# The shift of the second norm added on TensorE for two token tiles, and a routing product moved to ScalarE

## The chip, the cores and the metric

The kernel runs on one core of a Trainium2 chip. The metric is the device time of one execution in microseconds (us). Five engines run their own instruction streams in order and wait for one another through semaphores: TensorE (PE, with its weight loads shown apart as PEld), VectorE (DVE), ScalarE (ACT), GpSimd (POOL) and SyncE (SP), which issues most DMAs. PE writes only to PSUM banks; DVE and ACT read them.

## What is computed

Two layers of an encoder over 1024 tokens of width 1024, all in float32. Each layer: a norm, a projection, attention and a linear recurrence side by side, an output projection with a gated residual; then a second norm, a router that picks two of 32 experts for every token, and the experts. The part that matters here, from the reference:

```python
x = x + gt1 * mixed
h2 = rms_norm(x, norm2_g[l]) * (1.0 + sc2) + sh2
x = x + gt2 * hier_moe(h2, moe_w_group[l], moe_b_group[l], moe_w_router[l], moe_b_router[l],
                       moe_w_gate[l], moe_w_up[l], moe_w_down[l])
...
g_top, g_idx = lax.top_k(g_prob, 1)
in_group = e_logits[jnp.arange(T), g_idx[:, 0]]
top_v, top_i = lax.top_k(in_group, TOP_K)
```

`sh2` is one row of 1024 numbers, the same for every token.

## The kernel before

The 1024 tokens are eight tiles of 128 tokens (tile 0 to 7), one token to a partition. In each layer a long stage, the mix (projection, attention, recurrence), is followed by the output projection and the routing (`out_proj`, L1350 on), and then by a loop over the experts (`moe`). This document speaks mostly of the stage between the mix and the experts, which runs once in each layer: about 930 to 1010 us in layer 0 and 2202 to 2283 us in layer 1.

In it the last output products (`out_product`, tile `po`, 24 matmuls into two PSUM banks for each tile and half of the inner dimension) are added to the residual `xm` by DVE (L1342), and ACT squares the sum for the norm (L1344). For each token tile `logits` transposes `xm` on PE (L1377, tile `n2_xT_ps`), ACT copies that to SBUF (L1378), PE multiplies by the router's weights (L1380, tile `pl`, 36 columns) and DVE copies the result to `lg` (L1381). `norms` makes the reciprocal root on DVE (L1385 and L100 to L109). `scale` finishes the logits (L1390, L1391). `finish` makes the normed row itself, `h2`: DVE multiplies (L1395), DVE adds the shift (L1396), and ACT's queue issues the DMA to `h2d` in DRAM (L1397). The shift needs no place in the logits, since `router_weights` folds it into their bias ahead of time.

Routing goes by four tiles at a time. `route_select` picks two experts for each token with some 25 short DVE instructions and two ACT exponentials (L1489, L1498); its result is the one-hot `r_oh`. `route_rank` counts tokens for each expert with two PE matmuls into `r_pc` (L1515, L1516), turns the counts into ranks (L1518, L1519), multiplies `r_oh` by the token codes and by the weights (L1522, both on DVE, tile `r_rhs`) and sums them with eight pairs of a DVE comparison (L1528, tile `r_ohr`, four buffers) and a PE matmul (L1529, tile `r_pv`); L1530 adds that to the table `r_tab`. `route_tables` turns the table into index lists (L1537 to L1541). Then POOL gathers the rows of the first expert from `h2d` (L1665), PE transposes them (L1673), and the expert loop begins.

Tiles 6 and 7 come last: their logits, norm and rows are made while the ranks of tiles 0 to 3 are still being made, and the selection and ranking of tiles 4 to 7 stand alone at the end.

PSUM: `tp` has two banks (transposes), `po` four (output products), `pl` two, which `pl`, `r_pc` and `r_pv` share in turn.

Order: each engine runs its instructions in the order in which a scheduler put them when the program was built. The scheduler takes the code's order as priority and places an instruction where its own estimate of the engines' times finds it ready. So an edit at one place can change the order elsewhere. In the expert loop the order is fixed by `in_order`.

Of the kernel before, what the change touches and what calls it, by code (L numbers as in the profile page):

```python
# [10 lines left out]
F32 = mybir.dt.float32  # L11
# [3 lines left out]
AF = mybir.ActivationFunctionType  # L15
OP = mybir.AluOpType
# [36 lines left out]
class Trunk:  # L53
# [1309 lines left out]
    def out_proj(self, l, side, psum, early, late):  # L1363

        nc, a = self.nc, self.a
        with ExitStack() as s:
            tp = s.enter_context(self.pool(name=f"tO{l}", bufs=2, side=side))
            wr, br = self.wr, self.br

            def logits(t):  # L1370
                pl = psum.tile([128, 36], F32, name="pl", tag="pl")
                xT = tp.tile([128, 8, 128], F32, name="n2_xT", tag="n2_xT")
                for g in range(2):
                    pt = psum.tile([128, 4, 128], F32, name="n2_xT_ps", tag="tp")
                    for k in range(4):
                        c = 512 * g + 128 * k
                        nc.tensor.transpose(pt[:, k, :], self.xm[:, t, c:c + 128], self.ident)  # L1377
                    nc.scalar.copy(xT[:, 4 * g:4 * g + 4, :], pt)  # L1378
                for k in range(NK):
                    nc.tensor.matmul(pl, xT[:, k, :], wr[:, k, :], start=(k == 0), stop=(k == NK - 1))  # L1380
                nc.vector.tensor_copy(self.lg[:, t, :], pl)  # L1381

            def norms(t, n):
                ss = tp.tile([128, n], F32, name="n2_s", tag=f"n2_s{n}")
                nc.vector.tensor_tensor(ss, self.ss[:, t:t + n, 0], self.ss[:, t:t + n, 1], op=OP.add)  # L1385
                return self.rsqrt(tp, ss, n, NORM_EPS, 1.0 / D, "n2")

            def scale(t, n, rs):
                lg = self.lg[:, t:t + n, :]
                nc.vector.tensor_tensor(lg, lg, rs.unsqueeze(2).to_broadcast([128, n, 36]), op=OP.mult)  # L1390
                nc.vector.tensor_tensor(lg, lg, br.unsqueeze(1).to_broadcast([128, n, 36]), op=OP.add)  # L1391

            def finish(t, rs):
                h2 = tp.tile([128, D], F32, name="h2", tag="h2", bufs=4)
                nc.vector.scalar_tensor_tensor(h2, self.xm[:, t, :], rs, self.g2, op0=OP.mult, op1=OP.mult)  # L1395
                nc.vector.tensor_add(h2, h2, self.sh2)  # L1396
                nc.scalar.dma_start(self.h2d[128 * t:128 * t + 128, :], h2)  # L1397

            self.route_init(self.mx)
            early()  # L1400
            parts = self.out_parts(psum, [(t, 0) for t in range(4, NT)])

            def more(n):
                for _ in itertools.islice(parts, n):
                    pass

            more(4)
            for t, n in enumerate((4, 4, 5, 5)):
                logits(t)
                more(n)  # L1410
            rs = norms(0, 4)
            scale(0, 4, rs)
            for t in range(4):
                finish(t, rs[:, t:t + 1])
                if t == 1:
                    logits(4)
                    more(10)
            logits(5)
            rs = norms(4, 2)
            scale(4, 2, rs)  # L1420
            self.route_select(0, tp)
            more(99)
            self.route_rank(0, tp, psum)
            for i in range(2):
                finish(4 + i, rs[:, i:i + 1])
            logits(6)
            logits(7)
            late()
            rs = norms(6, 2)
            scale(6, 2, rs)  # L1430
            self.route_select(4, tp)
            for i in range(2):
                finish(6 + i, rs[:, i:i + 1])
            self.route_rank(4, tp, psum)
            pool = self.mx
            self.idx_s = pool.tile([128, 48], I32, name="idx_s")
            self.idx_g = pool.tile([128, 48], I32, name="idx_g")
            self.wsl = pool.tile([128, 48], F32, name="wsl")
            self.ovf = pool.tile([1, 16], I32, name="ovf")
            self.routed = self.route_tables(self.R["tab"], slice(0, 32), tp)  # L1440
# [65 lines left out]
    def route_rank(self, t, w, psum, k=4):  # L1506

        nc, R = self.nc, self.R
        tt = slice(t, t + k)
        oh = w.tile([128, k, 32], F32, name="r_sum", tag="r_sum", bufs=1)  # L1510
        nc.vector.tensor_add(oh, R["oh"][:, tt, 0, :], R["oh"][:, tt, 1, :])
        for i in range(k):
            nc.vector.tensor_add(R["acc"][:, t + i + 1], R["acc"][:, t + i], oh[:, i])
        pc = psum.tile([128, k, 32], F32, name="r_pc", tag="pl")
        nc.tensor.matmul(pc, R["ups"], oh, start=True, stop=False)  # L1515
        nc.tensor.matmul(pc, R["ones"], R["acc"][:, tt, :], start=False, stop=True)  # L1516
        tmp = w.tile([128, k, 2, 32], F32, name="r_tmp", tag="r_tmp", bufs=1)
        nc.vector.tensor_tensor(tmp, R["oh"][:, tt], pc.unsqueeze(2).to_broadcast([128, k, 2, 32]), op=OP.mult)  # L1518
        nc.vector.tensor_reduce(R["rk"][:, tt, :].unsqueeze(3), tmp, axis=AX.X, op=OP.add)  # L1519
        rhs = w.tile([128, k, 2, 64], F32, name="r_rhs", tag="r_rhs", bufs=1)  # L1520
        for j, n in enumerate(("code", "wt")):
            nc.vector.tensor_tensor(rhs[:, :, :, 32 * j:32 * j + 32], R["oh"][:, tt],  # L1522
                                                    R[n][:, tt].unsqueeze(3).to_broadcast([128, k, 2, 32]), op=OP.mult)
        pv = psum.tile([128, 64], F32, name="r_pv", tag="pl")
        for i in range(k):
            for c in range(2):
                ohr = w.tile([128, 128], F32, name="r_ohr", tag="r_ohr", bufs=4)
                nc.vector.tensor_scalar(ohr, R["io"], R["rk"][:, t + i, c:c + 1], None, op0=OP.is_equal)  # L1528
                nc.tensor.matmul(pv, ohr, rhs[:, i, c, :], start=(i + c == 0), stop=(i + c == k))  # L1529
        nc.vector.tensor_add(R["tab"], R["tab"], pv)  # L1530
# [472 lines left out]
```

## Time and profile before

| | us |
|---|---|
| median of 3 runs | 2689.37 |
| the runs | 2685.37, 2689.37, 2702.67 |
| the profiled execution, its own time | 2696.09 |
| its span from first to last instruction | 2694.1 |
| PE busy / DVE busy / ACT busy over the span | 2389.1 / 1852.7 / 1193.2 |

A row of a timeline gives start, duration, engine, line, operation, output and inputs with the size, how many instructions it merges, and in brackets how long the engine was idle before it and what released it. One float32 matmul of the program shows as two records of PE. [...] PE's instructions overlap, so that a row's duration is longer than the distance from its start to the next start.

### The profile page before, as it was taken

The numbers are of one execution on the slowest core, as the hardware profiler recorded it, in microseconds if no ns is written. First come the engines' busy times: TensorE is split into PE (matmuls) and PEld (weight loads), VectorE is DVE, ScalarE is ACT, GpSimd is POOL, SyncE is SP. The second block draws the span as 40 slices with busy tenths as digits, with TensorE's granted clock in tenths as the row PEclk, the third lists the DMA queues.
The fourth block names the chain that finished last, engine by engine and source line by source line (L and its number), as shares of the span: only waits on it lengthen the run. The fifth ranks groups of instructions, "written<-read, shape, count | busy, mean of one in ns | idle before, by whom it ended". The sixth has DMA issues, their size and how long they took to land. (4 is left out here: it accounts for less than half of the span.)

```text
span 2694.1 us, 45448 instructions
## 1 busy us (share of the span) xinstructions
PE 2389.1 (89%) x17313; PEld 1826.6 (68%) x17313; DVE 1852.7 (69%) x4053; ACT 1193.2 (44%) x2316; POOL 313.7 (12%) x251
## 2 busy tenths in 40 slices
PE   6999998898889979999959989989997996999992
PEld 3666666777767866777736767767776885677771
DVE  4347767656579486877764588965658847787775
ACT  3344443234256224555545555424426622555552
POOL 3100000000000002333310000000000001333330
PEclk8998998789989979999979989899988997999996
DMA  8566765525354247999942434445336325899985
GB/s 295 175 214 205 211 210 166 155 91 148 93 171 126 95 171 290 354 338 359 369 174 103 147 113 143 141 140 166 117 89 193 104 97 195 319 385 348 336 307 202
DMA packets 263940, 542.68 MB, mean 201 GB/s; under 512 B 76504, under 2 KB 180896, under 8 KB 234784
## 3 DMA queue, kind: packets, MB, share of 16 engines
q1 hardware_dynamic: 235712, 484.61, 53.9%
q0 software_dynamic: 23376, 40.99, 4.1%
q10 hardware_dynamic: 4624, 14.06, 1.4%
q8 instruction: 141, 2.31, 0.4%
q14 instruction: 87, 0.71, 0.1%
HBM read 459.29 MB, written 120.09 MB: 215 GB/s over the span
## 5 line engine op out<-in xcount | busy, mean ns | idle before, releaser
L1646 DVE TENSOR_TENSOR w_lo<-w_gu,w_hi 128x2048 fp32r<-128x2048 f32 x134 | 306.3, 2286 | 69.2 <-ACT w_hi L1645 69.0
L1645 ACT CAST w_hi<-w_gu 128x2048 fp32r<-128x2048 f32 x134 | 255.7, 1908 | 211.2 <-PE h_ps L1698 204.5
L361 PE MATMUL pj<-hh,wa_hi 128*128 128x512 f32 x800 | 335.2, 419 | 2.1 <-ACT wa_hi L348 1.7
L362 PE MATMUL pj<-hl,wa_hi 128*128 128x512 f32 x800 | 332.2, 415 | 1.1 <-DVE hl L338 1.0
L363 PE MATMUL pj<-hh,wa_lo 128*128 128x512 f32 x800 | 325.5, 408 | 0.1
L1737 PE MATMUL y_ps<-w_d,hT 128*128 128x512 f32 x560 | 252.2, 593 | 3.4 <-ACTq L1798 2.4
L1697 PE MATMUL h_ps<-w_hi,xT_hi 128*128 128x512 f32 x560 | 243.0, 434 | 4.4 <-ACT xT_hi L1681 4.4
L1698 PE MATMUL h_ps<-w_hi,xT_lo 128*128 128x512 f32 x560 | 222.6, 398 | 2.5 <-DVE xT_lo L1682 2.5
L1699 PE MATMUL h_ps<-w_lo,xT_hi 128*128 128x512 f32 x560 | 222.4, 397 | 0.0
L1726 POOL DMA_INDIRECT yd<-yo,idx_s x70 | 183.6, 2623 | 290.2 <-DVE yo L1723 275.4
L361 PEld LDWEIGHTS pj<-hh,wa_hi 128*128 128x128 f32 x800 | 156.2, 195 | 41.5 <-issue 6.0
L362 PEld LDWEIGHTS pj<-hl,wa_hi 128*128 128x128 f32 x800 | 155.8, 195 | 37.0 <-issue 4.0
L363 PEld LDWEIGHTS pj<-hh,wa_lo 128*128 128x128 f32 x800 | 155.2, 194 | 35.4 <-issue 3.6
L1737 PEld LDWEIGHTS y_ps<-w_d,hT 128*128 128x128 f32 x560 | 100.9, 190 | 104.8 <-issue 100.4
L1697 PEld LDWEIGHTS h_ps<-w_hi,xT_hi 128*128 128x128 f32 x560 | 107.3, 192 | 38.0 <-issue 11.5
L1698 PEld LDWEIGHTS h_ps<-w_hi,xT_lo 128*128 128x128 f32 x560 | 107.3, 192 | 36.7 <-DVE th L1689 11.5
L1682 DVE TENSOR_TENSOR xT_lo<-xT_ps,xT_hi 128x1024 fp32r<-128x1024 f32 x70 | 85.7, 1225 | 65.8 <-ACT xT_hi L1681 65.8
L1699 PEld LDWEIGHTS h_ps<-w_lo,xT_hi 128*128 128x128 f32 x560 | 107.0, 191 | 23.0
L1723 DVE SCALAR_TENSOR_TENSOR yo<-y_ps,wsl,gt 128x1024 f32<-128x1024 f32 x70 | 89.8, 1283 | 38.3 <-PE y_ps L1737 38.3
L1192 ACT ACTIVATE at_p<-at_s,at_mx 128x256 f32<-128x256 f32 (+7 forms) x128 | 94.8, 741 | 40.6 <-DVE at_mx L1190 39.8
L1190 DVE TENSOR_REDUCE at_mx<-at_s 128x1 f32<-128x256 f32 (+7 forms) x128 | 95.6, 752 | 14.5 <-PE at_s L1188 13.3
L238 PE MATMUL ada_ps<-ada_w,crep 128*32 128x128 f32 x1536 | 71.9, 313 | 37.6 <-DMA ada_w<-in_ada_w 37.4
(436 smaller groups left out, 4949.3 us busy)
## 6 DMA issues: line engine op xcount, KB each, us to landing
w_gu<-in_moe_w_gu SPq DMA_DIRECT2D x140, 1024.0 KB
w_d<-in_moe_w_down SPq DMA_DIRECT2D x70, 1024.0 KB
ada_w<-in_ada_w SPq DMA_DIRECT2D x96, 512.0 KB
wa_raw<-in_w_in SPq DMA_DIRECT2D x50, 512.0 KB
sp_z<-z SPq DMA_DIRECT2D x32, 768.0 KB
b_zz<-sp_z SPq DMA_DIRECT2D x32, 512.0 KB
cy<-yd SPq DMA_DIRECT2D x16, 1024.0 KB
qkv<-qst SPq DMA_DIRECT2D x48, 256.0 KB
```

The costliest lines, as they stand in the source:

```text
L361: nc.tensor.matmul(ps, hi[:, k, :], self.hh[k][:, sl], start=(k == 0), stop=False)
L362: nc.tensor.matmul(ps, hi[:, k, :], self.hl[k][:, sl], start=False, stop=False)
L363: nc.tensor.matmul(ps, lo[:, k, :], self.hh[k][:, sl], start=False, stop=(k == NK - 1))
L1190: nc.vector.tensor_reduce(mx, ps[:, 0:n], axis=AX.X, op=OP.max, negate=True)
L1192: nc.scalar.activation(pm[:, 0:n], ps[:, 0:n], AF.Exp, bias=mx, accum_out=hs["s"][:, t, m:m + 1])
L1645: self.nc.scalar.copy(hi, raw)
L1646: eng.tensor_tensor(lo, raw, hi.bitcast(F32), op=OP.subtract)
L1697: nc.tensor.matmul(ph, hi[:, k, :], whi[:, k % 4, :], start=(k == 0), stop=False)
L1698: nc.tensor.matmul(ph, lo[:, k, :], whi[:, k % 4, :], start=False, stop=False)
L1699: nc.tensor.matmul(ph, hi[:, k, :], wlo[:, k % 4, :], start=False, stop=(k == NK - 1))
L1726: st = nc.gpsimd.indirect_dma_start(out=self.yd, out_offset=bass.IndirectOffsetOnAxis(ap=self.idx_s[:, e:e + 1], axis=0), in_=yos[e % 2], ...
L1737: nc.tensor.matmul(po[:, 512 * half:512 * half + 512], hT[:, k, :], w[:, k, 512 * half:512 * half + 512], start=(k == 0), stop=(k == 1))
```

## The change

Two edits, in both layers.

First, in `finish`: for tiles 6 and 7 DVE no longer adds the shift. For each half of 512 columns PE forms in a `po` bank the product of a row of ones and the row `sh2` (one partition deep), adds the product of the identity and `h2` to it, and ACT copies the bank back into `h2`.

Second, in `route_rank` for tiles 4 to 7: the product of the one-hot and the codes is made by eight ACT instructions of 128x32 in place of one DVE instruction of 128x256.

```diff
             def finish(t, rs):
                 h2 = tp.tile([128, D], F32, name="h2", tag="h2", bufs=4)
                 nc.vector.scalar_tensor_tensor(h2, self.xm[:, t, :], rs, self.g2, op0=OP.mult, op1=OP.mult)
-                nc.vector.tensor_add(h2, h2, self.sh2)
+                if t < 6:
+                    nc.vector.tensor_add(h2, h2, self.sh2)
+                else:
+
+                    for half in range(2):
+                        cs = slice(512 * half, 512 * half + 512)
+                        po = psum.tile([128, 512], F32, name="n2_h", tag="po")
+                        nc.tensor.matmul(po, self.R["ones"][0:1, :], self.sh2[0:1, cs], start=True, stop=False)
+                        nc.tensor.matmul(po, self.ident, h2[:, cs], start=False, stop=True)
+                        nc.scalar.copy(h2[:, cs], po)
                 nc.scalar.dma_start(self.h2d[128 * t:128 * t + 128, :], h2)
...
         for j, n in enumerate(("code", "wt")):
-            nc.vector.tensor_tensor(rhs[:, :, :, 32 * j:32 * j + 32], R["oh"][:, tt],
-                                                    R[n][:, tt].unsqueeze(3).to_broadcast([128, k, 2, 32]), op=OP.mult)
+            if t and n == "code":
+                for i in range(k):
+                    for c in range(2):
+                        nc.scalar.activation(rhs[:, i, c, 0:32], R["oh"][:, t + i, c, :], AF.Copy, scale=R[n][:, t + i, c:c + 1])
+            else:
+                nc.vector.tensor_tensor(rhs[:, :, :, 32 * j:32 * j + 32], R["oh"][:, tt],
+                                        R[n][:, tt].unsqueeze(3).to_broadcast([128, k, 2, 32]), op=OP.mult)
```

What the scheduler made of it. The text calls the new matmuls by ones and `sh2` the shift matmuls (L1403 after) and those by the identity the identity matmuls (L1404 after); the lines of the changed kernel are 9 to 14 higher from here on. First place, PE in layer 0 near the end of the output products, where `po_10316` and `po_10331` are the last two banks of products and `n2_xT_ps` is a transpose for tile 5. Before:

```order
L1336 MATMUL po_10331<-wo_0at_q0_9212,mT_10194 128x512
L1337 MATMUL po_10331<-wo_0at_q1_9213,mT_10194 128x512
L1377 MATMUL n2_xT_ps_10243<-ident_86,xm_8653 128x128 x4
L1338 MATMUL po_10316<-wo_0at_q0_9212,mT_10194 128x512
L1336 MATMUL po_10316<-wo_1at_k0_9274,mT_10194 128x512
```

After:

```order
L1336 MATMUL po_10331<-wo_0at_q0_9212,mT_10194 128x512
L1337 MATMUL po_10331<-wo_0at_q1_9213,mT_10194 128x512
L1403 MATMUL n2_h_10521<-sh2_8667,r_ones_9937 128x512
L1403 MATMUL n2_h_10525<-sh2_8667,r_ones_9937 128x512
L1377 MATMUL n2_xT_ps_10243<-ident_86,xm_8653 128x128 x4
L1338 MATMUL po_10316<-wo_0at_q0_9212,mT_10194 128x512
L1336 MATMUL po_10316<-wo_1at_k0_9274,mT_10194 128x512
```

The two shift matmuls of tile 6 now stand inside the last output products.

Second place, PE in layer 0 right behind the last output product: the transposes of tile 6 (`n_xT_ps`), the two count matmuls into `r_pc`, the rank matmuls into `r_pv`, and the logits `pl` of tile 6. Before:

```order
L1377 MATMUL n_xT_ps<-ident,xm 128x128 x8
L1515 MATMUL r_pc<-r_sum,r_ups 128x128
L1516 MATMUL r_pc<-r_acc,r_ones 128x128
L1529 MATMUL r_pv<-r_rhs,r_ohr 128x64 x7
L1380 MATMUL pl<-wr,n_xT 128x36 x3
```

After:

```order
L1377 MATMUL n_xT_ps<-ident,xm 128x128 x2
L1524 MATMUL r_pc<-r_sum,r_ups 128x128
L1377 MATMUL n_xT_ps<-ident,xm 128x128 x6
L1403 MATMUL n_h<-sh,r_ones 128x512
L1525 MATMUL r_pc<-r_acc,r_ones 128x128
L1543 MATMUL r_pv<-r_rhs,r_ohr 128x64 x4
L1380 MATMUL pl<-wr,n_xT 128x36 x4
```

Six transposes and a shift matmul of tile 7 now stand between the two count matmuls, and only four rank matmuls ahead of the first logits.

Third place, PE in layer 0 from there to the next count matmul: the last eight rows of `pl` are the logits of tile 7. Before:

```order
L1529 MATMUL r_pv<-r_rhs,r_ohr 128x64
L1380 MATMUL pl<-wr,n_xT 128x36
L1377 MATMUL n_xT_ps<-ident,xm 128x128 x4
L1380 MATMUL pl<-wr,n_xT 128x36 x4
L1377 MATMUL n_xT_ps<-ident,xm 128x128 x4
L1380 MATMUL pl<-wr,n_xT 128x36 x8
```

After:

```order
L1377 MATMUL n_xT_ps<-ident,xm 128x128 x4
L1543 MATMUL r_pv<-r_rhs,r_ohr 128x64
L1403 MATMUL n_h<-sh,r_ones 128x512
L1543 MATMUL r_pv<-r_rhs,r_ohr 128x64 x3
L1380 MATMUL pl<-wr,n_xT 128x36 x4
L1377 MATMUL n_xT_ps<-ident,xm 128x128 x4
L1404 MATMUL n_h<-h_10519,ident 128x512 x2
L1404 MATMUL n_h<-h_10530,ident 128x512 x2
L1380 MATMUL pl<-wr,n_xT 128x36 x8
```

The four identity matmuls stand ahead of the logits of tile 7. In layer 1 the order is the same but for two things: the last shift matmul stands one rank matmul later, and the logits of tile 7 are cut, four of the eight ahead of the first two identity matmuls, four between these and the last two.

On DVE the two additions (L1396) and one product (L1522 with `r_code`) of tiles 4 to 7 are gone, and the addition to `r_tab` for tiles 0 to 3 (L1530) moves: in layer 0 behind both multiplications of L1395, in layer 1 to the place before the last step of the root. On ACT four copies of 128x512 stand behind the `n2_xT` copies of tile 7, and the eight products stand four ahead of and four behind the exponential L1498.

Elsewhere the rows of every engine are the same rows. But on PE, DVE, ACT and SP those of layer 1's mix from about 1710 us of the profile to about 2000 us stand in another order, with groups of projection matmuls, recurrence steps and attention tiles interleaved in another way.

## Rows read from the trace of the kernel before

**Rows 1.** Windows: two of layer 1's routing stage, then one of layer 0's.

```profile
2202.00:2247.00 45.00, 44.71 (x281) 39.34 (x280) 34.79 (x95) 18.87 (x40) 0.00 (x0) 1.00 0.27 100
...
2258.00:2272.80 14.80, 5.27 (x20) 4.49 (x20) 11.28 (x50) 0.42 (x2) 0.90 (x1) 0.50 0.47 176
...
975.00:987.50 12.50, 10.33 (x58) 9.99 (x57) 9.73 (x31) 4.50 (x7) 1.05 (x2) 0.64 0.43 180
```

**Rows 2.** Timeline of DVE, layer 1, from the last output products to the table.

```profile
2246.01 0.69 DVE L1342 TENSOR_TENSOR xm<-xm,po 128x512 f32<-128x512 f32 x1
...
2247.38 0.42 DVE L1518 TENSOR_TENSOR r_tmp<-r_oh,r_pc 128x256 f32<-128x256 f32 x1 [0.35 <-PE r_pc L1516]
...
2248.29 1.77 DVE L1528 TENSOR_SCALAR r_ohr<-r_io,r_rk 128x128 f32<-128x128 f32 x8
2249.98 0.15 DVE L1385 TENSOR_TENSOR n_s<-n_ss 128x2 f32<-128x2 f32 x1
...
2253.04 2.48 DVE L1395 SCALAR_TENSOR_TENSOR h<-xm,rs_y_n,g 128x1024 f32<-128x1024 f32 x2
...
2255.54 2.35 DVE L1396 TENSOR_TENSOR h<-h,sh 128x1024 f32<-128x1024 f32 x2
2257.81 0.18 DVE L1381 COPY lg<-pl 128x36 f32<-128x36 f32 x1
```

**Rows 3.** Timeline of DVE, layer 1, the last ranking.

```profile
2264.02 0.42 DVE L1522 TENSOR_TENSOR r_rhs<-r_oh,r_code 128x256 f32<-128x256 f32 x1
2264.35 0.15 DVE L1504 TENSOR_TENSOR r_wt<-r_wt,r_ex 128x4 f32<-128x4 f32 x1
```

**Rows 4.** Timeline of POOL, layer 1: the first gather.

```profile
2272.83 2.43 POOL L1665 DMA_INDIRECT xg<-h2d,idx_g  x1 [13.93 <-DVE idx_g L1539]
```

**Rows 5.** Timeline of PE at the full clock: expert loop, then layer 1's routing.

```profile
1043.60 3.60 PE L1737 MATMUL y_ps<-w_d,hT 128*128 128x512 f32 x8
...
2245.57 0.40 PE L1338 MATMUL po<-wo_3at_v,mT 128*128 128x512 f32 x1
2245.81 1.04 PE L1377 MATMUL n_xT_ps<-ident,xm 128*128 128x128 f32 x8
...
2248.63 1.77 PE L1529 MATMUL r_pv<-r_rhs,r_ohr 128*128 128x64 f32 x14 [1.29 <-DVE r_ohr L1528]
...
2251.80 0.98 PE L1380 MATMUL pl<-wr,n_xT 128*128 128x36 f32 x8
```

**Rows 6.** Timeline of DVE, layer 0: the same places as in rows 2.

```profile
975.27 0.42 DVE L1518 TENSOR_TENSOR r_tmp<-r_oh,r_pc 128x256 f32<-128x256 f32 x1 [0.35 <-PE r_pc L1516]
...
979.66 0.22 DVE L1530 TENSOR_TENSOR r_tab<-r_tab,r_pv 128x64 f32<-128x64 f32 x1 [1.64 <-PE r_pv L1529]
...
982.61 2.47 DVE L1395 SCALAR_TENSOR_TENSOR h<-xm,rs_y_n,g 128x1024 f32<-128x1024 f32 x2
...
987.26 0.19 DVE L1381 COPY lg<-pl 128x36 f32<-128x36 f32 x1
```

**Rows 7.** Timeline of ACT: scaled copies of 128x64 in layer 0, layer 1's last exponential.

```profile
146.05 1.05 ACT L673 ACTIVATE arv<-id,P 128x64 f32<-128x64 f32 x4
...
2262.85 0.20 ACT L1498 ACTIVATE r_ex<-r_ex 128x4 f32<-128x4 f32 x1 [3.57 <-DVE r_ex L1497]
```

**Rows 8.** Timeline of PE, layer 0's routing, then first expert matmuls before the clock rose.

```profile
979.81 1.09 PE L1377 MATMUL n_xT_ps<-ident,xm 128*128 128x128 f32 x4
980.70 1.76 PE L1380 MATMUL pl<-wr,n_xT 128*128 128x36 f32 x8
...
996.88 3.68 PE L1529 MATMUL r_pv<-r_rhs,r_ohr 128*128 128x64 f32 x16 [1.29 <-DVE r_ohr L1528]
...
1026.68 0.63 PE L1699 MATMUL h_ps<-w_lo,xT_hi 128*128 128x512 f32 x1
1027.11 0.63 PE L1697 MATMUL h_ps<-w_hi,xT_hi 128*128 128x512 f32 x1
```

**Rows 9.** Windows, the stretch of layer 1's mix whose order changes.

```profile
1710.00:2000.00 290.00, 263.71 (x2862) 211.14 (x2861) 194.28 (x600) 110.22 (x278) 2.59 (x10) 0.93 0.47 139
```

## The prediction, made before the changed kernel was run

> **What bounds the kernel now.** I read the windows of the routing stage first, then DVE's timeline through it, then who waits there for whom. The end is set by different engines in turn. [...] Between 2258.00 and 2272.80 PE is busy 5.27 of 14.80 us and DVE 11.28 us; this is the selection and ranking of tiles 4 to 7, a chain of short DVE instructions with nothing beside it [rows 1]. The chain starts when the logits of tile 7 are copied to `lg`, at 2257.81 us [rows 2], and runs without a choice of order through the one-hot products [rows 3] to the first gather at 2272.83 us, which had waited 13.93 us for the index list [rows 4]. The gather's rows are then waited for by the first expert. So in each layer the time of the copy of tile 7's logits carries through to the end, and so does what lies behind it on DVE. What stands just ahead of that copy on DVE is the change's target: the two additions, started at 2255.54, keep DVE until 2257.81 [rows 2].
>
> **What it removes.** Two additions a layer: 2257.81 - 2255.54 = 2.27 us of DVE, all of it ahead of the copy. One product a layer: 2264.35 - 2264.02 = 0.33 us of the last chain [rows 3]. If nothing took their place this were 2.6 us a layer, 5.2 us in all.
>
> **What it adds, and where.** Eight float32 matmuls of 512 columns a layer. The nearest row is `y_ps`, eight records in 3.60 us: 0.45 us a record at most, and 0.43 when the overhang of the last one is taken off; two records a matmul, so 0.86 us each [rows 5]. I take the same for the shift matmuls, which are one partition deep: the columns are as many. Below, they could cost nothing if depth counted; that would take up to 2.6 us off each layer's sum.
>
> The first two shift matmuls stand inside the output products, where PE has no gap, so the last product ends 1.72 us later: 2245.57 becomes 2247.29, and DVE's last addition to `xm` goes from 2246.01 to 2247.7. Behind it the two count matmuls now have six transposes (eight in 1.04 with the overhang: 0.11 each, 0.66) and a third shift matmul (0.86) between them. PE starts its transposes at 2245.81 + 1.72 = 2247.53; two of them, a count matmul (two records of 128 columns, 0.22), six more, the shift matmul and the other count matmul with about 0.2 for its result to reach DVE make 0.22 + 0.22 + 0.66 + 0.86 + 0.44 = 2.40. So `r_tmp` starts at 2249.95 and not at 2247.38 [rows 2, 5]. In both layers the first ranking is 2.6 us later: comparisons from 2250.88 (2248.29 before), first rank matmul 0.34 behind, at 2251.22 (2248.63 before).
>
> Layer 1 from there, PE in its new order, full clock. A rank matmul is 0.23, four logits matmuls 0.81 to 0.85 (eight records in 0.98 with the overhang), four transposes 0.45: four rank matmuls to 2252.15, logits of tile 6 to 2253.0, transposes to 2253.45, three rank matmuls to 2254.1, shift matmul to 2255.0, the last rank matmul to 2255.2. DVE has its comparisons done at 2252.65 and the root up to its last step at 2254.8, and there it waits for the table's addition, to 2255.4, which now stands ahead of that step. The two multiplications start at 2255.8 and not at 2253.04. PE then does logits and transposes to 2256.5, four logits matmuls of tile 7 to 2257.35, two identity matmuls (the first multiplication ended at 2257.1) to 2259.07, the other four logits matmuls to 2259.9. The copy of tile 7's logits starts at 2260.1; before, 2257.81. **Plus 2.3 us, less 0.33: plus 2.0 us.**
>
> Layer 0. `r_tmp` moves from 975.27 to 977.86 likewise, the first rank matmul to 979.12. Here the table's addition no longer stands ahead of the multiplications, and with it goes a wait of 1.64 us [rows 6]; these start at 982.85, against 982.61. At the full clock PE does its pieces up to the second transposes of tile 7 by 984.4, then the four identity matmuls to 987.85, then eight logits matmuls (1.7) to 989.55. Copy at 989.75, before 987.26: **plus 2.5, less 0.33: plus 2.2 us.** DVE is emptied, and the logits now wait for PE, behind matmuls whose result nothing needs before the gather.
>
> The rest costs nothing. The ACT copies follow the identity matmuls, the last of which ends near 2261.6, and their DMA has until the gather, then at 2274.8: 13 us for two copies and 512 KB. If that cover went, the gather would wait by as much as is missing. The eight scaled copies: the nearest rows are four of 128x64 in 1.05 us, so four of 128x32 take 0.8 to 1.05. The first four start when the first one-hot is done and end about when the exponential is wanted, 2262.85 (delay 0 to 0.3 us a layer, I take 0); the last four end some 2 us ahead of their rank matmuls [rows 7].
>
> Sum: 2.2 + 2.0 = +4.2 us. Against the profiled execution's own time, 2696.1 us, this is 2700.3; that execution lies 6.7 us above the median of the three runs, 2689.4, and against the median I predict 2693.6, rounded 2694.
>
> **The rivals.**
>
> *The clock falls inside the new order (slower).* [...] Before the change this cost nothing, since DVE was later. Now it would: a rank matmul 0.46 (3.68 / 8), four logits matmuls 1.73, four transposes 0.89, a 512-column float32 matmul 0.80 to 0.86, twice (a record of the expert products is 0.43 apart at the lower level and 0.24 at the higher) [rows 5, 8]. Layer 0 from 979.12: 1.84 + 1.73 + 0.89 + 0.46 + 1.7 + 1.38 + 1.73 + 0.89 + 6.8 + 3.47 = 20.9, copy at 1000.2: +12.9, less 0.33. Layer 1 in the same way 17.5 from 2251.22, copy at 2268.9: +11.1, less 0.33. One layer so: about +14 in all, 2703; both: +23, 2713. For it: the idle ahead of the rank matmuls is as long as before. Against: three 512-column matmuls now stand near it, and layer 1 kept its clock. If it falls only later, the price lies between. [...]
>
> *The other side: layer 1's mix in its new order (faster).* Between 1710 and 2000 us PE is idle 290.00 - 263.71 = 26.3 us [rows 9]. The same rows stand there in another order, and PE is the busiest engine. If the new order fills more than 4.2 us of that idle, a sixth, the kernel ends faster than before; filling a third gives 2689.4 + 4.2 - 8.8 = 2685. It can as well open as much: 2702. Nothing in the order says which; what waits there is a recurrence with short steps on four engines.
>
> *The change brings what it takes off DVE.* 5.2 us less, 2684. This needs tile 7's logits not to wait for the identity matmuls. PE's rows stand in the trace in the printed order, so it holds only where these cost far less than the 0.86 of `y_ps`.
>
> **How the numbers follow.** Forecast with the full clock and a mix that moves by less than 4 us: 0.45. Clock lost in one layer 0.25, in both 0.08. Mix gains more than 4.2 us: 0.15. Intended gain 0.05; 0.02 for anything else. The single runs of before spread over 17 us, so even the median of a few moves by some us. The range: 2679 to 2714, from the mix filling over half of its idle to the clock lost in both layers; the forecast's own range is 2687 to 2701. One per cent is 27 us, about what a measurement of this kernel can tell from no change. Only the mix opening 20 us more together with a lost clock reaches it upwards (0.04), only a mix that fills nearly all its idle downwards (0.02).
>
> **What would show it.** After: last product's addition to `xm` 1.7 us later in the stage; `r_tmp` of the first ranking 2.6 us later; in DVE's timeline the copy of tile 7's logits with an idle ahead of it released by PE, some 4 us in layer 0 and 1.7 in layer 1, where before there was none; identity matmuls with records 0.43 apart (0.8 if the clock fell); first gather 2 to 2.5 us later against the start of the stage. The prediction is wrong if the stage from its first output product to the gather gets shorter, or if the stretch of the mix changes by more than 8 us.

## The result, and the profile after

The changed kernel is slower: 2718.4 us (median of six runs, 2707.1 to 2731.2) against 2694.7 for the kernel before beside it, a ratio of 1.0093 with an interval of 1.0071 to 1.0114. Two later measurements gave 1.0118 (1.0095 to 1.0141) and 1.0100 (1.0079 to 1.0122): 25, 32 and 27 us, not the 4 us of the forecast.

The profiled execution (2707.1 us, span 2705.2) hides it: before anything that the change touches, it is already 12.4 us ahead of the one of before, in instructions of the same order. So spans aren't compared here; stages are. A **stage** runs from the row wo_0at_q (L1336) of tile 7's first output product to the first gather. In PE's and POOL's timelines before, both ends in layer 0 and the start in layer 1 (its gather is in [rows 4]):

```profile
966.43 0.39 PE L1336 MATMUL po<-wo_0at_q,mT 128*128 128x512 f32 x1
...
1002.34 2.39 POOL L1665 DMA_INDIRECT xg<-h2d,idx_g  x1 [13.99 <-DVE idx_g L1539]
...
2238.51 0.40 PE L1336 MATMUL po<-wo_0at_q,mT 128*128 128x512 f32 x1
```

That is 35.9 us in layer 0 and 34.3 in layer 1. After:

```profile
954.01 0.40 PE L1336 MATMUL po<-wo_0at_q,mT 128*128 128x512 f32 x1
...
998.09 2.39 POOL L1679 DMA_INDIRECT xg<-h2d,idx_g  x1 [23.62 <-DVE idx_g L1553]
...
2241.28 0.39 PE L1336 MATMUL po<-wo_0at_q,mT 128*128 128x512 f32 x1
...
2286.30 2.44 POOL L1679 DMA_INDIRECT xg<-h2d,idx_g  x1 [21.22 <-DVE idx_g L1553]
```

The stages take 44.1 and 45.0 us: plus 8.2 and plus 10.7. DVE's timeline in layer 1, then layer 0, answers to [rows 2, 6]:

```profile
2253.42 0.42 DVE L1527 TENSOR_TENSOR r_tmp<-r_oh,r_pc 128x256 f32<-128x256 f32 x1 [1.88 <-PE r_pc L1525]
...
2261.26 0.22 DVE L1544 TENSOR_TENSOR r_tab<-r_tab,r_pv 128x64 f32<-128x64 f32 x1 [2.92 <-PE r_pv L1543]
2261.59 2.48 DVE L1395 SCALAR_TENSOR_TENSOR h<-xm,rs_y_n,g 128x1024 f32<-128x1024 f32 x2
...
2270.50 0.20 DVE L1381 COPY lg<-pl 128x36 f32<-128x36 f32 x1 [6.32 <-PE pl L1380]
...
2273.09 0.17 DVE L1508 TENSOR_REDUCE r_gs<-r_ge 128x4 f32<-128x16 f32 x1 [1.04 <-ACT r_ge L1498]
...
983.30 0.20 DVE L1381 COPY lg<-pl 128x36 f32<-128x36 f32 x1 [7.89 <-PE pl L1380]
```

Counted from the stage's start, layer 1's `r_tmp` is 3.3 us later than in [rows 2], tile 7's logits 9.9 us (2270.50 - 2241.28 = 29.2 against 2257.81 - 2238.51 = 19.3). DVE waits 6.32 and 7.89 us for PE ahead of that copy, where it waited for nothing. PE in layer 1:

```profile
2251.84 1.12 PE L1403 MATMUL n_h<-sh,r_ones 1*128 1x512 f32 x2
...
2254.67 1.10 PE L1543 MATMUL r_pv<-r_rhs,r_ohr 128*128 128x64 f32 x8 [1.29 <-DVE r_ohr L1542]
2255.61 1.03 PE L1380 MATMUL pl<-wr,n_xT 128*128 128x36 f32 x8
...
2258.53 2.07 PE L1403 MATMUL n_h<-sh,r_ones 1*128 1x512 f32 x2
...
2263.58 1.76 PE L1380 MATMUL pl<-wr,n_xT 128*128 128x36 f32 x8
2265.14 3.76 PE L1404 MATMUL n_h<-h,ident 128*128 128x512 f32 x4
2268.70 1.76 PE L1380 MATMUL pl<-wr,n_xT 128*128 128x36 f32 x8
```

Eight logits records take 1.03 us at 2255.61 and 1.76 at 2263.58; a shift matmul 1.12 and then 2.07. The windows say why (the stretch and its length; the busy time of PE, PEld, DVE, ACT and POOL with the count of instructions; the granted clock, 1.00 being the full one; the DMA engines' busy share; GB/s):

```profile
970.40:980.60 10.20, 10.20 (x27) 5.91 (x27) 3.37 (x7) 1.86 (x4) 1.90 (x2) 0.53 0.01 3
...
2257.30:2270.50 13.20, 13.20 (x44) 9.51 (x44) 3.75 (x12) 2.35 (x4) 1.90 (x2) 0.50 0.04 17
```

PE is busy all the time, in layer 1 at a granted clock of 0.50, and DVE runs 3.75 of 13.20 us: PE has become the bound of the stage. In layer 0 the clock is back at about 980.1 (0.50 from 970.00 to 980.00, 1.00 from 980.40), amid the identity matmuls, and that layer loses less.

### The profile page after: what moved, and what is told of

Read it like the earlier page. It is cut to its first block, busy times and chain, and to the rows that moved or that the text cites. A ratio compares the mean times of both kernels' runs of the same rounds, so it can differ in the third digit from the quotient of the medians.

```text
span 2705.2 us, 45536 instructions
## 1 busy us (share of the span) xinstructions
PE 2394.7 (89%) x17345; PEld 1820.7 (67%) x17345; DVE 1850.9 (68%) x4047; ACT 1204.1 (45%) x2340; POOL 314.5 (12%) x251
## 5 line engine op out<-in xcount | busy, mean ns | idle before, releaser
L1712 PEld LDWEIGHTS h_ps<-w_hi,xT_lo 128*128 128x128 f32 x560 | 106.6, 190 | 36.3 <-DVE th L1703 11.5
L1737 DVE SCALAR_TENSOR_TENSOR yo<-y_ps,wsl,gt 128x1024 f32<-128x1024 f32 x70 | 89.9, 1284 | 38.2 <-PE y_ps L1751 38.2
L1679 POOL DMA_INDIRECT xg<-h2d,idx_g x70 | 75.7, 1081 | 246.7 <-PE xT_ps L1687 201.2
```

Of the source, the lines that this page charges most:

```text
L1712: nc.tensor.matmul(ph, lo[:, k, :], whi[:, k % 4, :], start=False, stop=False)
```

## Experiments

The stages in all runs, in us. "Forms" names PE's order: P as before; L0 and L1 as in the changed kernel's layers; A all four identity matmuls ahead of tile 7's logits; F as L1, with the idle ahead of the rank matmuls filled (also in layer 0 of the run that fills both); B all new matmuls behind the logits; S as B, with one shift matmul in the idle. Ratio against before on the same chip.

| kernel | layer 0 | layer 1 | ratio (95%) |
|---|---|---|---|
| before | P 35.9 | P 34.3 | 1 |
| changed, three traces | L0 44.1, 44.1, 44.1 | L1 45.0, 45.6, 44.1 | 1.0093, 1.0118, 1.0100 |
| layer 1 only | P 35.8 | A 45.6 | 1.0026 (1.0005 to 1.0046) |
| layer 0 only, two traces | L0 44.1, 44.1 | P 35.2, 35.6 | 1.0040 (1.0025 to 1.0055), 1.0061 (1.0038 to 1.0084) |
| all behind the logits | B 42.0 | B 43.5 | 1.0041 (1.0020 to 1.0062) |
| codes only | P 35.2 | P 35.0 | 1.0075 (1.0053 to 1.0097) |
| before, idle filled, order kept | P 36.6 | P 33.6 | 0.9987 (0.9968 to 1.0007) |
| the same, order moved | P 35.8 | P 34.1 | 1.0061 (1.0037 to 1.0084) |
| one idle filled, layer 1 only | P 35.1 | F 39.3 | a single execution |
| changed, idle filled | F 41.0 | F 40.9 | 1.0045 (1.0029 to 1.0061) |
| changed, order kept, two traces | L0 44.1, 44.1 | A 39.1, 44.0 | 1.0053 (1.0035 to 1.0072), 1.0071 (1.0050 to 1.0092) |
| shift behind, both layers | S 40.3 | S 31.2 | 1.0027 (1.0006 to 1.0048) |
| shift behind, layer 1 | P 36.3 | S 40.2 | 0.9989 (0.9968 to 1.0009) |

### One layer at a time

```diff
-                if t < 6:
+                if t < 6 or self.l == 0:        # layer 1 only; self.l == 1 for layer 0 only
...
-            if t and n == "code":
+            if self.l == 1 and t and n == "code":      # self.l == 0 for layer 0 only
```

> Both edits in layer 1 only; layer 0's stage and layer 1's mix keep the order of before. The planner here puts all four identity matmuls ahead of tile 7's eight logits records on PE (the changed kernel had two, then half the logits, then two). The stage is read from the first output product of tile 7 to the first gather: before 35.9 us in layer 0 and 34.9 in layer 1, changed kernel 44.1 and 45.6. Theory Q (PE's queue at the lowered clock): layer 0 stays at 35.9; layer 1 takes at least 45.6, and up to 3.7 us more, since two identity matmuls (3.76 us for four records in the changed kernel) move ahead of the copy of tile 7's logits; the time is 10.5 to 14.5 us above before. If the clock stays at the full rate: stage at 34.9 + 2.0 + 1.9 = 38.8. Theory M (the loss of the changed kernel is the reordered mix of layer 1): the time is within 4 us of before.

> Both edits in layer 0 only. Layer 1's mix then stands in the changed kernel's order, layer 1's stage in that of before. Theory Q: layer 0's stage is 44.1 us (before 35.9), layer 1's 34.9, the stretch from layer 0's first gather to layer 1's first output product of tile 7 is that of before (1235.6 us) within its spread, and the time is 8 us above before. Theory M: that stretch is 1242 us again, as in the changed kernel, and the time is 15 us above before (8 of the stage and 7 of the mix).

Layer 1 alone: plus 7 us (1 to 12), its stage 45.6; layer 0 alone: plus 11 (7 to 15), stage 44.1. (These two expectations took layer 1's stage from a row 0.5 us ahead of wo_0at_q, hence 34.9 for 34.3 and 45.6 for 45.0.) The loss lies in the stages of both layers, as theory Q says. The times alone don't decide: layer 1's 7 us is below Q's 10.5 to 14.5, and its interval reaches both that and the 4 us of theory M's first case; layer 0's holds both the 8 and the 15 us. A run further on shows form A at 39.1 us where the clock is kept, so executions that lose less than the trace's 11.3 us are to be expected. Whether M adds something was left open here.

### Where the queue is, and what the clock does to it

```diff
+                    with self.tc.issue_after(self.last_pl.ins):     # last matmul of tile 7's logits
...
                         nc.tensor.matmul(po, self.R["ones"][0:1, :], self.sh2[0:1, cs], start=True, stop=False)
                         nc.tensor.matmul(po, self.ident, h2[:, cs], start=False, stop=True)
```

> The changed kernel with all eight new matmuls of a layer held behind tile 7's logits on PE, so that PE's order up to these logits is that of before; the same work is done. Theory Q: nothing waits for the new matmuls, and DVE is freed of the additions: r_tmp of the first ranking as before, tile 7's logits copied 2.3 us earlier in layer 1 (at PE's end of them) and some 0.5 us earlier in layer 0, where PE ended them only 0.7 us ahead of the copy; with 0.33 us of the product a layer the stages take 32.3 and 35.1 us, the time is 3 us below before, if layer 1's mix, which is in a third order here, moves by nothing. A rival (ACT): the copies of the results stand on ACT beside the exponentials and the scaled copies, and the store of the two tiles lands after the index list; then the gather waits for the store and the stage is no shorter than before. Theory M: the time differs from before by the mix's order, by several us in either direction, whatever the stages do.

Theory Q's gain did not come, and the wait is not the rival's, which was for the store. The profiled execution (2731.3 us) is the slowest of twelve, whose median is 2714.9: its stages lose 6.1 and 9.2 us, its stretch between them stands in yet another order, and together they are more than the median's 11 us (5 to 17). It shows the mechanism, not the mean. PE and then DVE, layer 1:

```profile
2280.42 3.47 PE L1380 MATMUL pl<-wr,n_xT 128*128 128x36 f32 x16
2283.82 2.07 PE L1404 MATMUL n_h<-sh,r_ones 1*128 1x512 f32 x2
```

```profile
2283.92 0.20 DVE L1381 COPY lg<-pl 128x36 f32<-128x36 f32 x1 [2.10 <-PE pl L1380]
...
2300.80 0.42 DVE L1528 TENSOR_TENSOR r_tmp<-r_oh,r_pc 128x256 f32<-128x256 f32 x1 [9.18 <-PE r_pc L1526]
```

The clock fell here too, ahead of tile 7's logits (sixteen records in 3.47 us; at full they take 1.87). Without the additions DVE is free 17.8 us behind the stage's start, where it was free at 19.3, and then waits 2.10 us for PE: the copy starts at 19.9. Behind it, the eight matmuls, 2.0 us each as in the changed kernel at 0.50, run past the selection, and DVE waits 9.18 us for the count matmuls behind them. The queue was moved, not removed.

The clock itself was tested by adding work, in layer 1 alone, ahead of the first rank matmul:

```diff
+        if self.l == 1 and t == 0:
+            px = psum.tile([128, 512], F32, name="n2_fill", tag="pl")
+            for n in (512, 128):
+                with self.tc.issue_after(fill.ins):                 # behind the count matmuls
+                    fill = nc.tensor.matmul(px[:, 0:n], self.ident, self.xm[:, 0, 0:n], start=True, stop=True)
...
```

> Both edits in layer 1 only, in the changed kernel's order of layer 1's stage, and in the idle of PE ahead of the first rank matmul (1.29 us) one float32 matmul of 512 columns and one of 128 that nobody reads. Theory C1 (this idle lets the clock fall and with it goes the extra cost of the stage): the clock stays at full through the identity matmuls; rank matmuls 0.23, identity records 0.48, stage of layer 1 at 34.3 + 2.0 + 0.5 = 37 us. Theory C2 (the narrow work, not this idle, lets it fall): the clock falls as before near the second transposes of tile 7, identity records take 0.94, stage 45 us as in the changed kernel. Theory W (the queue alone, no clock): the stage is 45 us at whatever clock.

PE of that run:

```profile
2259.77 1.25 PE L1530 MATMUL n_fill<-xm,ident 128*128 128x512 f32 x4
2261.32 1.07 PE L1549 MATMUL r_pv<-r_rhs,r_ohr 128*128 128x64 f32 x8 [0.30 <-DVE r_ohr L1547]
...
2268.01 3.39 PE L1404 MATMUL n_h<-h,ident 128*128 128x512 f32 x4
2271.23 0.98 PE L1380 MATMUL pl<-wr,n_xT 128*128 128x36 f32 x8
```

With 1.25 us of work that nobody reads the stage is 5.7 us shorter (39.3 against 45.0; the changed kernel's other traces have 45.6 and 44.1), in an otherwise equal order. The clock falls some 6 us behind the rank matmuls' start and not 2.0, and is back for the last logits (0.98 us for eight records; the mean from 2257.45 to 2272.25 is 0.88). A stage that changes with the clock excludes theory W. The same filler in both layers, with nine matmuls behind layer 0's last ranking that keep layer 1's mix in the order of before:

> The changed kernel with the idle ahead of the first rank matmul filled in both layers (one float32 matmul of 512 columns and one of 128 that nobody reads), and with nine such matmuls of 512 columns behind the last rank matmuls of layer 0, in PE's idle before the first expert: these make the planner keep layer 1's mix in the order of before. Theory C1 (the clock is lost to the idle ahead of the rank matmuls): stage of layer 1 as in the run with the filler in layer 1 alone, 39.3 us (45.0 without), stage of layer 0 about 40.5 (44.1 without), the time 8 to 12 us above before, where the changed kernel was 25 to 31 above. Theory W (queue alone): stages 44.1 and 45.0, time 18 us above before or more. The nine matmuls behind the rank matmuls may cost or give some 3 us: at half the clock they reach past the arrival of the first expert's rows, at full they save its products.

Stages 41.0 and 40.9, time plus 12 us (8 to 17): the stages' sum, 5.1 + 6.6 = 11.7, accounts for it. In layer 0 the planner used layer 1's order here, so that its 41.0 differs from 44.1 by the order too; all three filled stages lie below the three of L1 without filling (44.1 to 45.6).

The sharpest pair came unasked. "Layer 1 only" and the first run of "changed, order kept" have the same order in layer 1's stage (form A), and the clock fell in one and not in the other: 0.61 over the 14.90 us ahead of the copy of tile 7's logits against 1.00 over 11.90. PE from the identity matmuls, layer 1 only:

```profile
2260.53 5.62 PE L1404 MATMUL n_h<-h,ident 128*128 128x512 f32 x8
2265.99 1.87 PE L1380 MATMUL pl<-wr,n_xT 128*128 128x36 f32 x16
```

and with the order kept:

```profile
2263.86 3.60 PE L1404 MATMUL n_h<-h,ident 128*128 128x512 f32 x8
2267.29 1.87 PE L1380 MATMUL pl<-wr,n_xT 128*128 128x36 f32 x16
```

5.62 against 3.60 there, with the rank and logits matmuls ahead likewise; stages 45.6 and 39.1. So 6.5 us of this form's 11.3 are the clock, 4.8 the queue.

### The order of layer 1's mix

```diff
-                if t < 6:
+                if t < 8:                       # additions as before in every tile; the second edit stays
```

> The second edit alone: the products of the last four tiles' choices with their codes on ACT, the additions as before. PE's order in the stages is that of before. Theory Q: both stages shorter by 0.3 us (one product of 0.33 us leaves DVE), time within 1 us of before when layer 1's mix, again in another order, moves by nothing. Rival: the exponential queues behind the scaled copies on ACT and DVE waits for it, stage longer by up to 0.3 us. Theory M: the time differs from before by several us although nothing but 0.3 us a layer was changed.

Both stages are P, and from the copy of tile 7's logits to the gather they are 0.2 us shorter a layer (14.86 and 14.78 us, before 15.08 and 15.02). The time is 20 us (14 to 26) above before, though the edit itself gains a little. In the trace the stretch from layer 0's gather to layer 1's stage takes 1252.1 us, 12.5 above the mean of nine executions in the order of before (below); the rest of the 20 is not placed, since the profiled execution is the fastest of its six (2698.6, median 2718.5).

The two kernels with PE's idle filled differ by one matmul, which lies in that idle, and by the order:

```diff
-            x = self.busy(psum, self.last_pl, 5 if self.l else 3)   # order kept
+            x = self.busy(psum, self.last_pl, 5 if self.l else 4)   # order moved
```

> The kernel before, with no edit of the change, and with float32 matmuls of 512 columns whose result nobody reads in PE's idle of the last ranking: behind tile 7's logits (three in layer 0, five in layer 1) and behind the last rank matmul (four and six). Every engine's order is that of before otherwise, layer 1's mix included. Theory C (the clock is lost to idle and narrow work, and half of what a later step costs there is the clock): the granted clock returns to full within the fillers, the eight rank matmuls take 1.9 us and not 3.68, the first expert's products 0.23 us each and not 0.43; the stage is 0.5 to 1.5 us shorter, the first expert some 4 us shorter, the time 5 to 12 us below before. Rival: the fillers run at half the clock, 2 us each, end behind the count matmul's operands (five take 10 us, the idle is 9.2), and the time is 0 to 8 us above before.

> The kernel above with one filler more in layer 0 (four and not three behind tile 7's logits), which lies in an idle of PE. The planner now puts layer 1's mix in another order, nearly that of the kernel with the second edit alone. Theory M (the order of layer 1's mix has a price of its own): 10 to 20 us above the kernel with three fillers, all of it between 840 and 1050 us behind layer 0's first gather, where the kernel with the second edit alone took 199 us from the first attention product to the last projection and before 188. If orders are worth nothing: the same time within 3 us.

2694.5 and 2712.1 us, 0.9987 and 1.0061: the order alone is worth 17.5 us. Their gathers of layer 0 start at 1005.89 and 1005.65, so the traces can be laid side by side; the last projection record of the mix, order kept and then moved:

```profile
2032.47 0.39 PE L363 MATMUL pj<-hh,wa_lo 128*128 128x512 f32 x1
```

```profile
2047.10 0.39 PE L363 MATMUL pj<-hh,wa_lo 128*128 128x512 f32 x1
```

14.9 us when counted from the gathers: 6 have come by the first attention product (at 840 and 846 us behind the gather), the other 9 up to here; 0.8 is added later. That is not all in the stretch that the expectation named.

Behind e6's matmuls the clock is up: layer 1's last rank matmuls take 2.00 us against 3.68 (as in [rows 8]; 0.50 there), and its stage is 0.7 us shorter, but layer 0's is 0.7 longer. The clock falls again ahead of the first expert's products, which are 0.43 us apart as before, and the total is level with before (0.9987, interval over 1).

The changed kernel again, and side by side with its two takings-apart:

> The changed kernel once more, beside the two runs below and the kernel before on one chip. So far the time is 0.93% above before (25 us), while its two layers changed one at a time gave +7 and +11 us. Theory S (stages, the order of layer 1's mix being worth nothing in this kernel): +19 us, the sum of the two stages (44.1 against 35.9 us in layer 0, 45.0 against 34.3 in layer 1, both read from the first product row wo_0at of tile 7). Theory M (the order of layer 1's mix adds to it): +25 us. The stages read as in the first trace in either case, 44.1 and 45.0 us.

> The changed kernel with ten float32 matmuls of 512 columns that nobody reads behind the last rank matmuls of layer 0, in PE's idle before the first expert; with them the planner keeps layer 1's mix in the order of before (layer 1's stage then has all four identity matmuls ahead of tile 7's logits, as in the run of layer 1 alone). Stages 44.1 and 45.6 us. Theory S plus M (stages, and the rest is the mix's order): 18 to 21 us above before, some 6 to 10 below the changed kernel; the stretch from layer 0's first gather to layer 1's last tile at 1236 to 1243 us as in the runs with this order. If something else of the change costs the rest: 25 to 31 us above before, as the changed kernel.

> The changed kernel beside the two runs below on one chip. Stages 44.1 and 45 us. If the mix's order has a price: 25 to 32 us above before again, 6 to 13 us more than the stages' 19. If the second measurement was an outlier of its executions: 19 to 25 us.

> Both edits in layer 0 only, once more; the mix of layer 1 in the changed kernel's order, layer 1's stage as before. If the order has a price of 6 to 13 us: 14 to 21 us above before (stage of layer 0 8.2), and the changed kernel 11 us above it. If it has none: 8 to 9 us above before.

> The changed kernel with the mix in the order of before (ten matmuls that nobody reads behind the last rank matmuls of layer 0), once more. If the mix's order has a price of 6 to 13 us: 14 to 19 us above before, by whether layer 1's stage keeps its clock (39.1 us) or not (45.6). If it has none: the same as the changed kernel within 3 us, or 6.5 us below it where the clock of layer 1's stage differs.

On one chip: changed plus 27 us (21 to 33), layer 0 only plus 16 (10 to 23), order kept plus 19 (14 to 25; its stages' sum is 17.8). The order costs 27 - 19 = 8 by the medians of the last pair, whose intervals overlap. By the traces, from layer 0's gather to layer 1's stage: nine executions in the order of before take 1236.2 to 1242.6 us, mean 1239.6; five in the order of the changed kernel 1241.5 to 1249.9, mean 1245.1. That is 5.5 us, and the ranges overlap by a little. It arises where the orders part. Up to the last rows that both have in common (`rb_m`, 704 us behind the gather) the groups are 1.2 us apart; from there to the first attention product the nine take 133.9 to 139.3 us, mean 136.3, the five 138.6 to 145.6, mean 141.9; from that product to layer 1's stage 399.1 and 397.9. Three executions in three other orders (all behind the logits, codes only, idle filled with the order moved) take 1252 to 1254.

So the sum of the change is 8.2 + 10.7 + about 6 = 25 us, against 25, 32 and 27 measured. The 32 (26 to 38) isn't fully placed; the profiled execution of that measurement reached layer 0's stage at 973.3 us, where before did at 966.4, so part of its excess lies ahead of anything that the change touches. Nor is the 10.7 exact: layer 1's stage in the order of before took 34.3, 35.2 and 35.6 us in three traces.

### A form that might win

> Both edits in both layers in another form: one shift matmul (0.96 us) in PE's idle ahead of the first rank matmul (1.29 us), the other three and the four identity matmuls behind tile 7's logits, and nine matmuls that nobody reads behind the last rank matmuls, to keep the clock for the first expert. Layer 1's mix keeps the order of before. Theory C1: the clock stays at full through tile 7's logits and, with the seven matmuls behind them, through the ranking; logits copied 2 us earlier than before in layer 1 and about 1 us in layer 0, the seven matmuls end (6.8 us) as the count matmuls are wanted, eight rank matmuls 1.9 us and not 3.68; stages about 33.5 and 31.5 us (35.9 and 34.3 before), first expert 2 to 4 us shorter, the time 5 to 14 us below before. Rival: the clock falls all the same, the seven matmuls take 13 us and the count matmuls wait for them, as with all eight behind the logits (stages 42.0 and 43.5 us there): 10 us above before or more.

> The form of the run before (one shift matmul in the idle ahead of the rank matmuls, the other seven matmuls behind tile 7's logits, products with the codes on ACT, nine matmuls that nobody reads behind the last rank matmuls) in layer 1 only, where it took the stage from 34.3 to 31.2 us and the first experts up to the count of all tiles from 44.3 to 40.3. Layer 0 is as before, with four matmuls that nobody reads behind the last rank matmuls. Layer 1's mix keeps the order of before. If layer 1 keeps its clock as there: 3.2 + 4.0 + 1.2 = 8 us below before. If the clock falls ahead of the seven matmuls, as in layer 0 there (stage 40.3 against 35.9): 2 to 5 us above before. Which of the two comes may differ from execution to execution; then the median lies between.

In the first of these layer 1 kept its clock and layer 0 did not, with PE in the same order up to the seven matmuls and with the same seven behind them; in the second layer 1 lost it. Windows of the stages, layer 0 and 1 of the first:

```profile
975.86:1016.15 40.29, 38.67 (x150) 26.30 (x149) 25.90 (x111) 14.49 (x28) 1.91 (x3) 0.68 0.39 141
2257.13:2288.28 31.15, 28.95 (x150) 20.57 (x149) 26.14 (x111) 14.08 (x28) 1.91 (x3) 0.93 0.52 194
```

and layer 1 of the second:

```profile
2232.93:2273.14 40.21, 38.59 (x152) 25.35 (x151) 25.82 (x111) 14.49 (x28) 1.90 (x2) 0.70 0.38 141
```

DVE of that layer 1 at its full clock:

```profile
2271.63 2.48 DVE L1395 SCALAR_TENSOR_TENSOR h<-xm,rs_y_n,g 128x1024 f32<-128x1024 f32 x2
2274.02 0.29 DVE L1381 COPY lg<-pl 128x36 f32<-128x36 f32 x2
```

Both last tiles' logits are copied right behind the multiplications: tile 7's some 17 us behind the stage's start (2274.02 - 2257.13 = 16.9 for the first of the two), 2.3 sooner than before. This is the gain that the change was built for. 31.15 us, at a mean of 0.93, is 3.2 below before and within 0.4 of the expectation; at 0.70 layer 1's same rows take 9 us more: 3.5 ahead of the copy, where DVE waits 2.71 us for the logits, and 5.6 behind it, mostly for the count matmuls (6.34), which stand behind the seven matmuls. The time of the second, 0.9989 (0.9968 to 1.0009), is no gain that can be shown. No version here beats before.

## Why the prediction was wrong, by its own steps

- **The chain: right.** The copy of tile 7's logits carries through to the gather. Layer 1: 9.9 later at the copy, 10.7 at the gather. Layer 0: 8.5 and 8.2.
- **What is taken from DVE: right in size, due only at the full clock.** The products with the codes were put at 0.33 us a layer; 0.2 was measured with that edit alone. The additions' 2.27 us come out in full where PE has the logits ready, as in the one stage of form S at the full clock (2.3). Where the clock has fallen, the logits wait for PE even without a new matmul ahead of them (2.10 us with all of them behind). The gain asks for both: no identity matmuls ahead of the logits, which the prediction said, and the full clock, which it did not.
- **`r_tmp` 2.6 us later: 3.3 measured, in both layers.** A record of a shift matmul was taken at 0.43 us; at the full clock two matmuls (four records) measure 1.98, 0.48 to 0.50 each. One partition deep, they were not cheaper here than the identity matmuls, 128 deep, whose eight records took 3.60 (order kept), 0.45 each.
- **The full clock through the new order: this is the step that failed.** The forecast, 0.45, had PE at the full clock up to tile 7's logits in both layers, plus 4.2 us, with a mix that moves by less than 4; the rival of both layers had 0.08. Of the ten traces of a stage with L0 or L1 in it (seven of layer 0, three of layer 1), all lost the clock ahead of these logits, and the stages cost 8.2 and 10.7 us, not 2.2 and 2.0. The working at the full clock was near: of form A one in three kept it, and there 34.3 + 2.0 for layer 1 + 1.9 for two more identity matmuls ahead makes 38.2 us, against 39.1 measured; 0.7 of the 0.9 is `r_tmp`.
- **The rival's price: right in layer 1, too high in layer 0.** Put at 12.6 and 10.8 us net a layer, measured 8.2 and 10.7. In both layers of this trace the first rank matmuls and the first logits of tile 6 still ran at the full clock, some 2 us cheaper than put. In layer 0 the clock also came back amid the identity matmuls, which take 5.68 us and not 6.8, and the logits behind them take 1.87 and not 3.47:

```profile
975.87 5.68 PE L1404 MATMUL n_h<-h,ident 128*128 128x512 f32 x8
981.39 1.87 PE L1380 MATMUL pl<-wr,n_xT 128*128 128x36 f32 x16
```

  Layer 1 comes so close by luck in part: the later `r_tmp` and a wait for ACT, below, made up for the 2 us. The kernel's two other traces have plus 11.2 and 9.7.
- **What spoke against the rival** was that three 512-column matmuls stand near the idle ahead of the rank matmuls, and that layer 1 had kept its clock. That the idle and such matmuls bear on the clock was the author's guess, which the trace of before doesn't show. The first did not hold the clock: it fell 2.0 us behind the start of layer 1's rank matmuls, 2.4 in layer 0, where it had fallen 2.1 us behind it before the change (1.00 up to 978.40, 0.50 from 978.60). With that idle filled in layer 1 it fell some 6 us behind. The second was read from a single trace. With PE in the order of before up to tile 7's logits, three of six traces of layer 1's stage lost the clock ahead of them. One is that of layer 0 only, second trace, where the logits take what they take in layer 0 [rows 8]:

```profile
2277.71 1.76 PE L1380 MATMUL pl<-wr,n_xT 128*128 128x36 f32 x8
2279.28 1.09 PE L1377 MATMUL n_xT_ps<-ident,xm 128*128 128x128 f32 x4
2280.16 3.47 PE L1380 MATMUL pl<-wr,n_xT 128*128 128x36 f32 x16
```

  In the changed kernel's layer 1 the clock was not soon back either: it stayed at 0.50 through 13.20 us in which PE was busy throughout. What brings it down and back is not shown by these runs.
- **ACT: one wait was missed.** The copies of the results were costed at nothing as far as the gather's cover goes, which holds. But they share ACT with the selection's exponential: in the first trace of the changed kernel the third copy of layer 1 starts at 2272.36, the exponential behind it at 2272.84, and DVE waits 1.04 us (row `r_gs` above). Layer 0 has no such wait, nor has layer 1 in the two other traces, where the last identity matmuls run at the full clock (1.96 us for four records). The scaled copies delayed nothing, as taken.
- **The mix: the right suspicion, and the loss left without a chance of its own.** The prediction had the new order able to gain or lose, and gave 0.15 to a gain over 4.2 us, but to a loss only 0.04, for one of 20 us beside a lost clock. It costs about 6.
- **The range** (to 2714) ended at the lost clock in both layers with a mix that moves by nothing; both came at once.

## What to carry to other kernels

Before work is moved to TensorE because it is idle there, ask at which clock it will run and what stands behind it in its queue: here matmuls of 0.96 us at the full clock cost 2.0 at 0.50, ahead of a result that the next engine waited for. Price the order that the planner makes of the whole program apart from the edit, with a second kernel that differs only in that order; here it was worth up to 17.5 us, nearly as much as the two stages lost (18.9). And where spans of one kernel vary by more than the change, compare stages between fixed rows.

## What was not expected of the hardware

- The clock isn't a property of the program alone. The same PE order of a stage took 39.1 and 45.6 us (form A), 31.2 and 40.2 (form S), by when 0.50 was granted in it (form A: 1.00 and 0.61 on average ahead of the copy of tile 7's logits; form S: 0.93 and 0.70 over the stage). In form L0 the fall in layer 0 came 15.1 to 15.9 us behind the stage's start in seven traces, so its moment varied there too, and the stage did not: 44.05 to 44.10 in all seven.
- The clock fell without any long idle: none ahead of the fall in the changed kernel's layer 1 is over 1.29 us, and PE then stayed at 0.50 through 13.20 us in which it was busy throughout.
- Useless work can pay: with 1.25 us of matmuls in an idle of 1.29 a stage was 5.7 us shorter. With a shift matmul of 1.12 us in the same idle the clock was kept in one of form S's three stages (0.93 over the stage) and not in the two others (0.68 and 0.70). What makes the difference stays open.
- Instructions in the same order, from the program's start to layer 0's stage, took 954 to 976 us in different executions. What moves them was not looked into.
